# Hybrid DeltaNet and dilated-attention layer: the second half's buffers re-laid, output weight rows and the heads' K loads re-timed

## The chip, the cores and the metric

The kernel runs on one core of a Trainium2 chip. The metric is the device time in microseconds (us) of one execution; lower is better. All data are float32 in memory.

## The reference, cut to what matters

A layer on 2048 tokens of width 1024. One normalised input feeds a projection whose columns go to two mixers, a gated delta rule (4 heads of 128, chunks of 64) and a dilated sliding-window attention (8 heads of 64, three patterns); both are gated, joined, and go through one output projection into the residual stream.

```python
def hybrid_layer(x, norm_w, w_in, conv_w, a_log, dt_bias, dn_norm_w, q_norm_w, k_norm_w, rel_bias, w_out):
    h = rms_norm(x, norm_w)
    qkv_dn, z_dn, b_dn, a_dn, qkv_att, gate_att = jnp.split(h @ w_in, cuts, axis=-1)
    y_dn = deltanet_branch(qkv_dn, z_dn, b_dn, a_dn, conv_w, a_log, dt_bias, dn_norm_w)
    y_att = dilated_attention_branch(qkv_att, gate_att, q_norm_w, k_norm_w, rel_bias)
    return x + jnp.concatenate([y_dn, y_att], axis=-1) @ w_out

# attention, per pattern (window, dilation) in ((128, 1), (512, 4), (2048, 16)):
#   p = softmax(q k^T + bias) over a band of window/dilation keys, stride dilation; o = p v
# the three patterns' outputs are combined by their softmax denominators, times silu(gate)
```

## The kernel before

**Stages.** First come the normalisation, the projections and convolutions of the delta rule, and the inverses of its chunk matrices (up to about 450 us); then the delta rule, beside the attention's projections; from about 1010 us on attention itself. Every float32 product is made of three matmuls on a high and a low part (`xh`/`xl`, `wh`/`wl`, `mhh`/`mhl`): an operand is split by ScalarE (the high part, a rounding copy) and then VectorE (the low part, the difference).

**Attention in steps.** 96 steps are recorded by `step(t, gen, n)`: eight groups of 12 steps, one for each pair of heads and half of the queries, `G[0]` to `G[7]`; groups 4 to 7 (steps 48 to 95) are the second half and read all 2048 keys. A step records the scores of step t (PE `sc<-K,qz`; VectorE adds the bias and finds the minimum, `pr<-sc,bias`; ScalarE takes the exponentials `pr<-pr,ml`), the turning of the probabilities of step t-1 (PE `pt`, copied to `pT` by VectorE and ScalarE), every second step the products with the values (PE `pv<-pT,V`), and between them some matmuls of a filler. The filler is `proj_fill` (the last projections, PE `pj`) up to step 47, and `out_fill` (the output projection, PE `po<-xh,mhh` and so on) from step 48 on. `out_fill` takes its work in jobs of 24 matmuls; each starts with a `yt` tile (the delta rule's output for 128 tokens) or an `mt` tile (attention's), which PE turns and ScalarE and VectorE split into `mhh` and `mhl`.

**Loads of a group.** `load()` of a group asks for its `q1` (0.5 MB), its keys `k1` (in the trace K; 1 MB in the second half) and two `bias` tiles. It is recorded four steps before the group starts, at its second place (`at_step(b - 4, 1, ...)`). `keys(pat)` copies K into a strided tile C on GpSimd. The values come as tiles V of 256 KB, by `vload`, at fixed places of the steps.

**Output weights.** `w_out` has eight rows of blocks (128x1024, 512 KB each). Rows 0 to 3 belong to the delta rule's half: `w_out_load(k)` loads them into the two `wraw` buffers in the last projection set of `proj_fill`, rows 0 and 1 at its column block `o8 == 1`, row 2 at 4 and row 3 at 5, when a split has freed a buffer; `wo_split` splits row k at `o8 == 4 + k`. Rows 4 to 7 are asked for at the start of `out_fill`, into two `res` buffers and the two halves of the tile K1, and split while the first two jobs run.

**Buffers.** At step 48 the pools of the projections are closed and the pool `wo` opens on the same bytes; its tiles are laid out in the order in which they are first asked for: `res` (3), C1, `yt` (2), K1, then `mhh`, `mhl`, `mt`. A tile on bytes that an earlier tile had waits for the last reader of those.

**Order.** From the attention on all instructions are recorded through a small helper (line L99 in the profile) that pins each engine's instructions to the order in which the code is written. SP issues nearly all DMAs, in that order; ScalarE issues some (`qk<-qs`, `v_d<-t`). The DMAs of both take eight completion semaphores in turn, so each issue also waits for the transfer that had its semaphore eight DMAs earlier, whatever it carried.

## Time and profile before

| | |
|---|---|
| median of 3 runs | 1446.1 us (1442.88 to 1447.8) |
| the profiled execution | 1442.2 us |
| its span in the trace | 1440.4 us |
| mean granted TensorE clock | 0.987 |
| busy: PE / VectorE / ScalarE / GpSimd | 1374.0 / 897.2 / 680.1 / 427.2 us |
| moved by DMA | 205.00 MB, mean 142 GB/s |

A row of a timeline gives the start, the duration, the engine and the operation, and in brackets how long the engine was idle before it and what ended that. SPq and ACTq rows are the issuing of DMAs by those engines; how long a transfer takes to land is told by the chain of waits. PE is busy nearly all the time, so what matters are its few idle stretches and the stretches in which its granted clock is the lower of its two levels (1.2 instead of 2.4 GHz). Times of different stretches are all of one execution and add up.

### The profile page before, as it was taken

What the parts mean: (1) busy time and instruction counts of PE and PEld (TensorE: products, weight loads), DVE (VectorE), ACT (ScalarE), POOL (GpSimd) and SP (SyncE); (2) the same over time, 40 slices, a digit from 0 to 9 for tenths busy, and PEclk for the clock granted to TensorE, in tenths of its full rate; (3) what the DMA queues carried; (4) which work ended last, traced back from release to release, by engine and by line L of the source; (5) the groups of instructions that cost most, each with busy time, mean ns of one, the idle gap of its engine ahead of it and who ended that gap; (6) DMA issues with size and microseconds to landing.
All of it is one profiled execution on the core that took longest, in us unless ns stands there. A gap on an engine that the chain in (4) does not pass through costs nothing.

```text
span 1440.4 us, 28745 instructions
## 1 busy us (share of the span) xinstructions
PE 1374.0 (95%) x10234; PEld 1223.6 (85%) x10234; DVE 897.2 (62%) x2786; ACT 680.1 (47%) x1937; POOL 427.2 (30%) x499
## 2 busy tenths in 40 slices
PE   7999999999998998999999899999998999999988
PEld 7998777777877887999999889999887778888877
DVE  6526678799894365777777554544354645466455
ACT  7634436642221333444444476665555545555520
POOL 0000000000002112442432523657466274655500
PEclk9999999999999999999999999999998999999999
DMA  7653445773557556566554554464448574755764
GB/s 218 165 117 70 99 102 133 156 132 55 116 88 193 147 83 171 133 166 168 133 143 76 124 127 116 100 174 119 112 118 246 146 247 134 216 154 171 200 175 150
DMA packets 301154, 205.00 MB, mean 142 GB/s; under 512 B 149283, under 2 KB 271027, under 8 KB 300500
## 3 DMA queue, kind: packets, MB, share of 16 engines
q1 hardware_dynamic: 233924, 171.70, 48.6%
q10 hardware_dynamic: 67088, 31.47, 7.9%
q8 instruction: 81, 1.33, 0.4%
q14 instruction: 61, 0.50, 0.1%
HBM read 142.61 MB, written 60.50 MB: 141 GB/s over the span
## 4 chain that ended last, share of the span: by engine, by line
PE 61%; DVE 15%; DMA 11%; ACT 5%; issue 4%; POOL 2%; SPq 1%; ACTq 0%; DVEq 0%; POOLq 0%
PE pj L99 13%; PE po L99 8%; PE pz L99 5%; PE sc L99 5%; PE pj L206 4%; PE pj L207 4%; PE pj L208 4%; PE pv L99 3%; PE pt L99 3%; DVE cy L473 3%; DVE inv L540 2%; DMA kT<-cv 2%; PE C L714 2%; PE SU L720 2%; ACT pr L99 2%
## 5 line engine op out<-in xcount | busy, mean ns | idle before, releaser
L99 ACT ACTIVATE pr<-pr,ml 128x192 f32<-128x192 f32 (+2 forms) x384 | 156.8, 410 | 161.6 <-DVE ml L99 161.6
L99 PE MATMUL pj<-wh,xh 128*128 128x256 f32 (+1 forms) x776 | 227.7, 293 | 0.0
L99 PE MATMUL pj<-wl,xh 128*128 128x256 f32 (+1 forms) x776 | 227.6, 293 | 0.0
L99 PE MATMUL pj<-wh,xl 128*128 128x256 f32 (+1 forms) x776 | 225.8, 291 | 0.0
L208 PE MATMUL pj<-xh,wl 128*128 128x512 f32 x512 | 203.9, 398 | 3.6 <-DVE wl L192 3.6
L206 PE MATMUL pj<-xh,wh 128*128 128x512 f32 x512 | 203.9, 398 | 1.3 <-ACT cy L475 1.2
L207 PE MATMUL pj<-xl,wh 128*128 128x512 f32 x512 | 203.2, 397 | 0.0
L99 PEld LDWEIGHTS pj<-wl,xh 128*128 128x128 f32 x776 | 148.3, 191 | 0.6 <-issue 0.4
L99 PEld LDWEIGHTS pj<-wh,xl 128*128 128x128 f32 x776 | 148.3, 191 | 0.0
L99 PEld LDWEIGHTS pj<-wh,xh 128*128 128x128 f32 x776 | 148.1, 191 | 0.2
L99 DVE CUSTOM_DVE_ANT_0 pr<-sc,bias 128x192 f32<-128x192 f32 (+2 forms) x384 | 100.1, 307 | 71.0 <-PE sc L99 70.2
L208 PEld LDWEIGHTS pj<-xh,wl 128*128 128x128 f32 x512 | 96.6, 189 | 27.3 <-DVE wl L192 5.3
L206 PEld LDWEIGHTS pj<-xh,wh 128*128 128x128 f32 x512 | 96.8, 189 | 24.4 <-ACT cy L475 1.6
L473 DVE SCALAR_TENSOR_TENSOR cy<-cu,cw,cy 128x512 f32<-128x512 f32 x144 | 107.9, 752 | 15.2 <-ACT cy L471 13.6
L207 PEld LDWEIGHTS pj<-xl,wh 128*128 128x128 f32 x512 | 96.6, 189 | 21.9
L99 POOL COPY qz<-q 64x512 f32<-64x512 f32 x96 | 92.5, 964 | 57.7 <-PE sc L99 54.7
L657 POOL MEMSET at__4520<- 64x256 f32 x1 | 0.3, 304 | 354.5 <-PE pj L207 354.5
L99 DVE COPY pT<-pt 64x128 f32<-64x128 f32 (+2 forms) x220 | 69.3, 323 | 56.4 <-PE pt L99 53.1
L99 PE MATMUL po<-xh,mhh 128*128 128x512 f32 x212 | 88.8, 419 | 3.9 <-ACT mhh L99 3.9
L99 PE MATMUL pv<-pT,V 128*64 128x128 f32 (+1 forms) x1328 | 79.1, 269 | 9.8 <-DVE pT L99 4.7
L99 PE MATMUL po<-xl,mhh 128*128 128x512 f32 x212 | 88.1, 415 | 0.0
L99 PE MATMUL po<-xh,mhl 128*128 128x512 f32 x212 | 87.7, 414 | 0.3 <-DVE mhl L99 0.3
(360 smaller groups left out, 3151.8 us busy)
## 6 DMA issues: line engine op xcount, KB each, us to landing
wraw<-in_w_in SPq DMA_DIRECT2D x44, 512.0 KB, 6.9
cv<-cy ACTq DMA_DIRECT2D x48, 256.0 KB, 2.7
Fb<-F SPq DMA_DIRECT2D x64, 192.0 KB, 5.7
xr<-in_xT SPq DMA_DIRECT2D x32, 256.0 KB, 4.5
kT<-cv SPq DMA_DIRECT2D x32, 256.0 KB, 3.3
qk<-qs ACTq DMA_DIRECT2D x64, 128.0 KB, 3.3
res<-in_x SPq DMA_DIRECT2D x13, 512.0 KB, 5.2
V<-v_d SPq DMA_DIRECT2D x20, 256.0 KB, 6.2
```

The lines of the kernel that those rows point to most:

```text
L99: i = f(*args, **kw)
L206: nc.tensor.matmul(ps, wh[:, k, c * P:(c + 1) * P], xh[tb][:, kt, :], start=kt == 0, stop=False)
L207: nc.tensor.matmul(ps, wh[:, k, c * P:(c + 1) * P], xl[tb][:, kt, :], start=False, stop=False)
L208: nc.tensor.matmul(ps, wl[:, k, c * P:(c + 1) * P], xh[tb][:, kt, :], start=False, stop=kt == KT - 1)
L473: nc.vector.scalar_tensor_tensor(y, u[:, i:i + 512], cw[:, ct, i:i + 1], y, op0=ALU.mult, op1=ALU.add)
L540: nc.vector.tensor_tensor(pr_[:, :i, :i], Tt[:, :i, :i], L[:, None, :i, i].to_broadcast([P, i, i]), op=ALU.mult)
L657: nc.gpsimd.memset(at_[:CH, :, :CH], 0.0)
L714: nc.tensor.matmul(pc[:, s_], g["WQ"][:, u, s_], S0[:, s_], start=True, stop=True)
L720: nc.tensor.matmul(su[:, s_], g["Ks"][:, u, s_], VN, start=True, stop=True)
```

## The change

```diff
@@ start of the pool mid2
+    mid.tile([P, 512], F32, name="t0", bufs=2)
     rs0 = [mid.tile([P, 512], F32, name="big", bufs=3) for _ in range(2)]
     for i in range(2):
         dma(rs0[i], dap(rstd_d, i * 512, [[0, P], [1, 512]]))
@@ def wo_split(kt, raw)
         if kt < 4:
-            nc.scalar.mul(wh, raw, dnw)
-            nc.vector.scalar_tensor_tensor(wl, raw, dnw, wh.bitcast(F32), op0=ALU.mult, op1=ALU.subtract)
+            for i, r in enumerate(raw):
+                n = r.shape[1]
+                h, l = wh[:, i * n:(i + 1) * n], wl[:, i * n:(i + 1) * n]
+                nc.scalar.mul(h, r, dnw)
+                nc.vector.scalar_tensor_tensor(l, r, dnw, h.bitcast(F32), op0=ALU.mult, op1=ALU.subtract)
@@ def w_out_load(k)
-        r = wp.tile([P, 4, 260], F32, name="wraw", bufs=2).rearrange("p a b -> p (a b)")[:, :1024]
-        dma(r, w_out[k * P:(k + 1) * P, :])
-        return r
+        if k == 2:
+            rs = [mid.tile([P, 512], F32, name="big", bufs=3) for _ in range(2)]
+        else:
+            rs = [wp.tile([P, 4, 260], F32, name="wraw", bufs=2).rearrange("p a b -> p (a b)")[:, :1024]]
+        n = D // len(rs)
+        for i, r in enumerate(rs):
+            dma(r, w_out[k * P:(k + 1) * P, i * n:(i + 1) * n])
+        return rs
@@ def proj_fill()
                     if o8 == 1:
-                        rs = [w_out_load(k) for k in range(2)]
+                        rs = [w_out_load(k) for k in range(3)]
                     if o8 == 4:
                         wo_tiles(0)
                     if o8 >= 4:
                         wo_split(o8 - 4, rs[o8 - 4])
-                        if o8 < 6:
-                            rs.append(w_out_load(o8 - 2))
+                        if o8 == 4:
+                            rs.append(w_out_load(3))
@@ for i, g in enumerate(G): b = 12 * i
         if i:
-            at_step(b - 4, 1, g["load"])
+            at_step(*((b - 4, 1) if i < 4 else (b - 3, 0) if i == 4 else (b - 3, 2)), g["load"])
@@ def ring_mh()
-        return [wo.tile([P, 4, P], F32R, name="mh" + c, bufs=3) for c in "hl"]
+        t = wo.tile([P, 2, 4, P], F32R, name="mh", bufs=3)
+        return [t[:, 0], t[:, 1]]
@@ ahead of out_fill
+    wo.tile([P, 512], F32, name="mt", bufs=2)
+    C1 = wo.tile([P, S], F32, name="C1")
+    loaded = {i: half_load(Q2[i], "dn", 4) for i in range(2)}
     RAW = [wo.tile([P, D], F32, name="res", bufs=3) for _ in range(2)]
-    C1 = wo.tile([P, S + 80], F32, name="C1")[:, :S]
-    loaded = {i: half_load(Q2[i], "dn", 4) for i in range(2)}
-    K1 = wo.tile([P, S + 48], F32, name="K1")[:, :S]
+    K1 = wo.tile([P, S + 150], F32, name="K1")[:, :S]
@@ def out_fill()
-        for k in range(4):
+        def raw_load(k):
             dma(RAW[k], w_out[(4 + k) * P:(5 + k) * P, :])
+
@@ after the first job's split
+        raws = {(0, 1): (raw_load, 0), (0, 2): (raw_load, 1), (0, 12): (raw_load, 2), (0, 22): (raw_load, 3)}
+        for k, at_ in enumerate(((0, 20), (1, 8), (1, 20), (2, 8))):
+            raws[at_] = (lambda k=k: wo_split(4 + k, RAW[k]),)
@@ in the loop over a job's matmuls
-                    if nth < 2 and m in (8, 16):
-                        k = 2 * nth + m // 8 - 1
-                        wo_split(4 + k, RAW[k])
+                    if (nth, m) in raws:
+                        f, *args = raws.pop((nth, m))
+                        f(*args)
```

Five things change. (1) In the pool `mid2` the tile `t0` is laid first, so the two `rstd` loads at about 445 us go to other bytes. (2) Row 2 of `w_out` is loaded in two halves into `big` buffers, together with rows 0 and 1; row 3 is asked for at `o8 == 4`; the split of row 2 is two instructions on each engine. (3) The loads of groups 4 to 7 are recorded later: at step b-3 instead of b-4, for groups 5 to 7 at its third place. (4) The pool `wo` is laid in another order: `mt`, C1, `yt`, `res`, K1, and `mhh` and `mhl` become two halves of one tile `mh`. (5) Rows 4 to 7 are asked for and split at given matmuls of the first three jobs, the loads at matmuls 1, 2, 12 and 22 of the first job, the splits at 20 of the first, 8 and 20 of the second and 8 of the third. The order on PE and on GpSimd is the same before and after.

On SP's queue, around the end of `proj_fill` and the start of `out_fill`, before:

```order
L99 DMA wraw<-in_w_out 128x1024
L99 DMA q_12380<-qk_76 128x1024
L99 DMA K_8182<-qk_80 128x2048
L99 DMA bias<-bs_d 64x3x192 x2
L99 DMA mx_d<-gt 128x256
L99 DMA wraw<-in_w_out 128x1024
L99 DMA mx_d<-gt 128x256
L99 DMA V<-v_d 64x4x128 x2
L99 DMA mx_d<-gt 128x256
L99 DMA yt<-y_d 128x512 x2
L99 DMA V<-v_d 128x5x128
L99 DMA res<-in_w_out 128x1024 x2
```

The same place after:

```order
L99 DMA wraw<-in_w_out 128x1024
L99 DMA mx_d<-gt 128x256
L99 DMA q_12421<-qk_76 128x1024
L99 DMA K_8183<-qk_80 128x2048
L99 DMA bias<-bs_d 64x3x192 x2
L99 DMA mx_d<-gt 128x256
L99 DMA V<-v_d 64x4x128 x2
L99 DMA mx_d<-gt 128x256
L99 DMA yt<-y_d 128x512 x2
L99 DMA V<-v_d 128x5x128
L99 DMA yt<-y_d 128x512
L99 DMA ml_90<-mr 96x2x64
```

The one `wraw` load left is row 3, in row 2's old place; K stands one DMA later; the loads of rows 4 and 5 (`res<-in_w_out`) leave their place behind the first V for one three issues later, out of this piece.

On SP's queue, at the load of group 5 (q_13221 and K_12638 are its `q1` and K), before:

```order
L99 DMA V<-v_d 128x4x128
L99 DMA q_13221<-qk_77 128x1024
L99 DMA K_12638<-qk_81 128x2048
L99 DMA bias<-bs_d 64x3x192 x2
L99 DMA acc_d<-res 128x1024
L99 DMA mx_d<-gt 128x256
L99 DMA res<-in_x 128x1024
L99 DMA V<-v_d 128x4x128
L99 DMA mx_d<-gt 128x256
```

The same place after:

```order
L99 DMA V<-v_d 128x4x128
L99 DMA acc_d<-res 128x1024
L99 DMA mx_d<-gt 128x256
L99 DMA res<-in_x 128x1024
L99 DMA V<-v_d 128x4x128
L99 DMA q_13306<-qk_77 128x1024
L99 DMA K_12644<-qk_81 128x2048
L99 DMA bias<-bs_d 64x3x192 x2
L99 DMA mx_d<-gt 128x256
```

The group's four loads now stand behind the store of `acc_d`, the load of `res` and the V of the last values of group 4. Groups 6 and 7 move in the same way.

On VectorE, around the split of the last `w_out` row in the first jobs, before:

```order
L99 ISA pr,ml<-sc,bias 128x192
L99 ISA ml 128x1
L99 TENSOR_TENSOR xl_12663<-K_12638,xh_12662 128x1024
L99 COPY pT_8741<-pt 128x2x128
L99 COPY pT_8741<-pt 64x128 x2
```

The same place after:

```order
L99 ISA pr,ml<-sc,bias 128x192
L99 ISA ml 128x1
L99 COPY pT_8742<-pt 128x2x128
L99 COPY pT_8742<-pt 64x128 x2
L99 TENSOR_TENSOR xl_12665<-K_12644,xh_12664 128x1024
```

A split of a weight row that stood ahead of the copies to `pT` stands behind them; it is the split of row 7 before and of row 6 after, since each split comes about one step later.

## Rows read from the trace of the kernel before

**Rows 1.** The page, part 1: busy time, share of the span, instructions

```profile
PE 1374.0 (95%) x10234; PEld 1223.6 (85%) x10234; DVE 897.2 (62%) x2786; ACT 680.1 (47%) x1937; POOL 427.2 (30%) x499
```

**Rows 2.** Windows: stretch, its length, busy time by engine, clock, DMA share, GB/s

```profile
1080.00:1100.00 20.00, 16.97 (x154) 16.12 (x154) 8.72 (x34) 12.40 (x41) 13.02 (x16) 0.95 0.86 241
1100.00:1120.00 20.00, 17.11 (x90) 14.61 (x90) 9.40 (x37) 10.87 (x36) 13.11 (x6) 0.80 0.73 234
1160.00:1180.00 20.00, 16.70 (x125) 14.32 (x122) 5.87 (x26) 7.10 (x29) 15.65 (x17) 0.83 1.01 337
```

**Rows 3.** Timeline of PE, 1095 to 1113: start us, us, operation [idle before <-releaser]

```profile
1096.34 0.66 PE L99 MATMUL pv<-pT,V 128*64 128x128 f32 x8 [3.03 <-DVE pT L99]
...
1100.34 1.90 PE L99 MATMUL sc<-K,qz 128*128 128x192 f32 x8
...
1104.78 1.09 PE L99 MATMUL po<-cs,yt 128*128 128x128 f32 x4 [2.22 <-DMA yt<-y_d]
1106.54 0.79 PE L99 MATMUL po<-xh,mhh 128*128 128x512 f32 x1 [0.67 <-ACT mhh L99]
```

**Rows 4.** Timeline of ACT and its DMA queue, 1088 to 1108

```profile
1092.76 0.37 ACTq L99 DMA_DIRECT2D v_d<-t  x1
1093.18 1.15 ACT L99 ACTIVATE xh<-wraw,dnw 128x1024 fp32r<-128x1024 f32 x1 [3.07 <-DMA K<-qk]
...
1103.91 0.54 ACT L99 COPY pT<-pt 64x128 f32<-64x128 f32 x2
1105.91 0.58 ACT L99 CAST mhh<-po 128x512 fp32r<-128x512 f32 x1 [1.45 <-PE po L99]
```

**Rows 5.** Timeline of SP's DMA issues, 1056 to 1112

```profile
1083.21 0.42 SPq L99 DMA_DIRECT2D K<-qk  x1
...
1100.57 0.80 SPq L99 DMA_DIRECT2D yt<-y_d  x2
```

**Rows 6.** Timeline of DVE, 1086 to 1108

```profile
1094.36 1.28 DVE L99 SCALAR_TENSOR_TENSOR xl<-wraw,dnw,xh 128x1024 fp32r<-128x1024 f32 x1 [6.01 <-ACT xh L99]
```

**Rows 7.** Timeline of DVE, 1126 to 1138

```profile
1136.02 1.23 DVE L99 TENSOR_TENSOR xl<-K,xh 128x1024 fp32r<-128x1024 f32 x1 [2.10 <-ACT xh L99]
```

**Rows 8.** Timeline of PE, 1130 to 1140

```profile
1137.96 1.19 PE L99 MATMUL pv<-pT,V 128*64 128x128 f32 x16 [1.03 <-DVE pT L99]
```

**Rows 9.** Chain that ended last, 1155 to 1185: start us, us, what

```profile
1156.52 6.23 DMA Fb<-F
...
1163.33 9.41 DMA res<-in_x
```

**Rows 10.** Timeline of SP's DMA issues, 1156 to 1182

```profile
1159.97 0.38 SPq L99 DMA_DIRECT2D K<-qk  x1
...
1164.01 0.69 SPq L99 DMA_DIRECT2D V<-v_d  x1
```

**Rows 11.** Timeline of PE, 1166 to 1182

```profile
1173.61 1.13 PE L99 MATMUL pv<-pT,V 128*64 128x64 f32 x16 [3.30 <-DVE res L99]
...
1178.57 2.04 PE L99 MATMUL sc<-K,qz 128*128 128x192 f32 x8
```

**Rows 12.** Timeline of SP's DMA issues, 1222 to 1246

```profile
1226.51 0.42 SPq L99 DMA_DIRECT2D K<-qk  x1
```

**Rows 13.** Timeline of POOL, 1230 to 1246

```profile
1236.75 3.88 POOL L99 COPY C<-K 128x2048 f32<-128x2048 f32 x1 [1.01 <-DMA K<-qk]
```

**Rows 14.** Timeline of PE, 1240 to 1246

```profile
1241.67 0.69 PE L99 MATMUL pv<-pT,V 128*64 128x64 f32 x16 [1.83 <-DMA V<-v_d]
...
1244.84 1.46 PE L99 MATMUL sc<-K,qz 128*128 128x192 f32 x8
```

**Rows 15.** The page, part 6: issues, KB each, median us to landing

```profile
V<-v_d SPq DMA_DIRECT2D x20, 256.0 KB, 6.2
```

**Rows 16.** Timeline of SP's DMA issues, 440 to 452

```profile
444.30 1.76 SPq L567 DMA_DIRECT2D big<-rstd_d  x2
...
447.59 0.46 SPq L99 DMA_DIRECT2D wraw<-in_w_in  x1
```

More of the change, by code (lines that the diff above doesn't have):

```diff
@@ L1384, in split @@
                 if buf not in spare:
-                    t = wo.tile([P, S + (80 if buf == "C1" else 48)], F32R, name=buf)[:, :S]
+                    t = wo.tile([P, S + (0 if buf == "C1" else 150)], F32R, name=buf)[:, :S]
                     t = t.rearrange("p (a b k c) -> p a b k c", a=2, b=2, k=4)
```

## The prediction, made before the result

> **What bounds the kernel now.** The page's first part comes first: TensorE (PE) is busy for 1374.0 us, 95% of the span [rows 1], so every engine that is slower by itself is hidden, and time can only come out of PE's idle stretches and out of the stretches at its lower clock. The table of windows shows where those lie in the second half: of three stretches of 20 us PE was busy 16.97, 17.11 and 16.70, with a granted clock of 0.95, 0.80 and 0.83 [rows 2]. Then the timeline of PE names each idle time and what ended it, and from there the chain of waits and the timelines of ScalarE, VectorE and SP are followed back to the transfer that was late. The stretches that the change touches have five such gaps: 3.03 us ahead of the values at 1096.34, 2.22 and 0.67 at the first output job [rows 3], 1.03 at 1137.96 [rows 8], 3.30 at 1173.61 [rows 11], 1.83 at 1241.67 [rows 14]. Together 12.1 us; the clock losses come on top. After gaps of 3.03 and 3.30 the clock falls to the lower of its two levels, 1.2 GHz; a drop can also be read at 1106 behind 2.22 and 0.67, and after 1.83 at 1241.67 none can: eight score matmuls take 2.04 us behind the gap of 3.30 and 1.46 behind that of 1.83 [rows 11, 14].
>
> **Part 1, the third weight row.** The gap at 1096.34 is a chain: PE waits for `pT` on VectorE, which stands behind the low part of row 2's split (1.28 us), which had been idle for 6.01 waiting for the high part on ScalarE [rows 6]; ScalarE was idle 3.07 us until the load of K, asked for at 1083.21, had landed [rows 4, 5]. ScalarE doesn't read K. In front of the split stands its own DMA issue `v_d<-t` at 1092.76 [rows 4], and by the turn of the eight semaphores that issue had K's. So it was not the weight that came late, but an issue that stood behind 1 MB on its semaphore. In the changed kernel one more DMA shifts the turn, and the store follows a small `mx_d` store on its semaphore, long landed; and row 2 is asked for with rows 0 and 1, three column blocks sooner. ScalarE then splits right behind its `t`, about 3 us earlier, and `pT` is ready when PE comes: −3.03. The clock drop behind the gap goes with it: 0.95 over 20 us is 0.05 × 20 = 1.0 us of full-rate work lost [rows 2]: −1.0. The second half-row costs one more instruction on ScalarE and VectorE; two pieces of half the length in the place of 1.15 and 1.28 us [rows 4, 6] add some tenths there, beside PE's filler: 0. As a DMA it is issued three column blocks before its use: 0. The Trainium skill ("DMA: Bandwidth & Descriptors", section Rules for kernel authors) asks for large transfers, 1 MiB and more, and speaks against the cut in two. No row here shows that a slower transfer would be felt at that place, so by it the sum would be the same.
>
> **Part 2, the start of the output job.** `yt` is asked for at 1100.57, when the last `pj` matmul has let its bytes go, and PE waits 2.22 us for it and 0.67 for the high part [rows 3, 5]. In the new layout `yt` no longer lies on bytes that this matmul reads, so SP asks as soon as the small stores ahead of it are out. What is late next is ScalarE: its exponentials of step 48 and the copies to `pT` end at 1103.91 + 0.54 = 1104.45, and the high part `mhh` takes 0.58 behind them [rows 4], so the first product can stand at about 1105.1 instead of 1106.54: −1.5. The bounds are 0 (ScalarE is as late as `yt` was) and 2.9 (both gaps go). An idle time of some 2.7 us behind the scores stays, so I let the clock drop there stay too.
>
> **Part 3, rows 4 to 7 later.** Their splits stand behind the copies to `pT`. At 1136.02 the low part (1.23 us) stood ahead of the copy that PE waited 1.03 us for [rows 7, 8]: −1.0. Against it, a split now stands ahead of the next scores' bias instead, and may delay those by its length: two such places are new, at most 1.2 each [rows 7], so +2.5 is the bound; PE has filler matmuls there, and I take 0. The rows are used from the seventh job on; their transfers have tens of us to land: 0. Of the eight semaphores their issues wait for loads before them, which costs SP time, not PE.
>
> **Part 4, K behind V.** At group 5, `res` was asked for behind K and took 9.41 us [rows 9]; V stood behind it at 1164.01 and landed when PE started at 1173.61 [rows 10, 11], 9.5 us for 256 KB against a median of 6.2 [rows 15]. The DMA engines were full (share 1.01, 337 GB/s [rows 2]). Here the trace agrees with a statement of the Trainium skill (the same page, section Queues, rings and completion order): each engine takes descriptors in ring order, so a small load waits behind the megabyte ahead of it. With `res` and V ahead of K both land before PE wants them: −3.30. The lower clock behind the gap goes: 0.83 over 20 us is 3.4 us of lost work, of which some 0.4 fell into the gap itself: −3.0 [rows 2]. The price: K is issued at about 1163.3 instead of 1159.97 [rows 10], since `q` ahead of it still waits, on its semaphore, for the `Fb` load that landed at 1156.52 + 6.23 = 1162.75 [rows 9]. From group 6, where K was issued at 1226.51 and GpSimd waited for it until 1236.75, it takes up to 10.2 us [rows 12, 13]: here 1172.2 to 1173.5. The scores that read it stand at 1178.57 [rows 11], and 6.3 sooner once gap and clock are gone: 1172.3. So PE waits 0 to 1.2 us: +0.5.
>
> At group 6, PE waited 1.83 for the V behind K [rows 14]: −1.8. K moves from 1226.51 to about 1232, lands at about 1242, and the scores at 1244.84 come 1.8 sooner, at 1243.0: covered, by 1 us. Group 7 is built alike and has no such gap: 0.
>
> **Part 5, `t0` first.** The second `rstd` load is the second half of the issue at 444.30, so at about 445.2; its new bytes wait for a store issued shortly ahead of it, which had landed by 447.59, when another issue that waited for it went out [rows 16]. The wait is between 0 and 447.59 − 445.2 = 2.4 us; behind it on SP stand the loads for which the delta rule's start already waits, so all of it would reach PE. I take +0.5: the store went out some us earlier, and I see nothing that waited for it before.
>
> **The sum**: −3.0 − 1.0 − 1.5 − 1.0 − 3.3 − 3.0 + 0.5 − 1.8 + 0.5 = −13.6 us. Against the profiled execution (1442.2, of it 1440.4 in the span) that is 1428.6; that execution lies 3.9 below the median of the three runs, and the sum counts equally from the median: 1446.1 − 13.6 = 1432.5.
>
> **The rivals.**
> - *The clock stays up at the output job too.* Speaks for it: the remaining idle time is shorter than the 2.22 + 0.67 and the wait for `pT` before it together. The window at 1100 to 1120 loses 0.20 × 20 = 4.0 us to the clock [rows 2], about 3 of them behind 1106: 1429.5. Chance 0.2.
> - *K is late at group 5.* The Trainium skill says on the same page (Rules for kernel authors, on overlap) to issue a DMA early and wait late; the change does the opposite with the largest load. As a mechanism of this kernel: K lands 12 us after its issue, because `res` and V (0.75 MB) stand right ahead of it in the same engines; PE waits 1163.3 + 12 − 1172.3 = 3.0 us, about as long as the gap that it removed, and the clock falls as it did behind that: 6.0 − 0.5 given back. 1432.5 + 5.5 = 1438. Against it: the longest landing of K in the rows is 10.2. Chance 0.18.
> - *Hardly any change.* K is late so at group 5 and group 6 (a landing of 13 us there, 2.0 of wait and 3.0 of clock): another 5 back, 1443; or the gap at 1096 stays, since the semaphore was not its cause and the copies stand behind something else. Chance 0.12.
> - *Slower.* K lands 16 us after its issue at all three group changes. PE waits 7.0, 5 and about 4 us, each with 3 us of lower clock: 25 lost, 0.5 of it in the sum already, against 13.6 gained: 1446.1 − 13.6 + 24.5 = 1457. The point from which it decides is where the three together lose more than 14 us: waits of 2 us and a clock drop at each, a landing of about 12.7 us. For it: engines at a share of 1.01 [rows 2]. Against it: V, `res` and K together are the same bytes as before, so K should land at about the time when V did, 1173.5. Chance 0.07.
> - *The early slip is at its bound* (2.4) and the splits delay scores by 2.5: +4.4, 1437; within the range.
>
> **How the numbers follow.** The forecast 0.43, the clock 0.2, K late once 0.18, hardly any change 0.12, slower 0.07. About 0.3% (4.3 us) is what can be told from no change: faster by more than that (below 1441.8) are the first three, 0.81; within it 0.12; slower 0.07. The range from the clock's case with its bounds (1429.5, less 2.9 − 1.5 for the whole of the output job's gaps, less the 3 us by which runs differ: 1425) up to just beyond K late once with half of the early bound (1438 and 2): 1440.
>
> **What would show it.** In the profile of the changed kernel: no idle time ahead of `pv` before step 48, and `v_d<-t` issued right behind `t`; `yt` issued ahead of the last `pj`, and the first product about 4.8 us behind the first scores of step 48; the granted clock of the stretch around group 5 at 1.00; `sc<-K` of steps 60, 72 and 84 with no wait for K of over 1 us; PE's waits at the start of the delta rule no longer than before. The forecast is wrong if `sc<-K` shows a wait with K as releaser, if the first `pv` of a group still waits for V or `res`, or if a gap of the same size stands at another place in the same step.

## The result, and the profile after

The changed kernel takes 1433.5 us in the median of 7 runs (1430.11 to 1440.55), the kernel before 1446.1 (1442.88 to 1449.67): a ratio of 0.993, with a 95% interval of 0.9906 to 0.9955. A second set of runs, side by side with other kernels, gave 1429.3 against 1442.9, a ratio of 0.9907 (0.9882 to 0.9933). The ratios here and below are those on record, each with its 95% interval; they are not quotients of the medians. The forecast was 1432.5.

The windows of the changed kernel (columns as in [rows 2]; the last row is the stretch of group 6):

```profile
1080.00:1100.00 20.00, 18.41 (x170) 17.29 (x168) 11.12 (x36) 13.63 (x44) 19.31 (x18) 1.00 0.85 258
1100.00:1120.00 20.00, 17.10 (x105) 14.46 (x107) 10.73 (x43) 10.40 (x36) 9.32 (x6) 0.91 0.67 187
1160.00:1180.00 20.00, 18.66 (x158) 15.70 (x158) 9.81 (x43) 10.88 (x42) 13.65 (x13) 1.00 0.97 305
1220.00:1240.00 20.00, 20.00 (x162) 17.13 (x162) 9.07 (x42) 10.33 (x41) 12.76 (x14) 1.00 0.87 274
```

Before, the first three stretches had PE busy for 16.97, 17.11 and 16.70 us at a clock of 0.95, 0.80 and 0.83. Two of the three clock losses are gone, PE was busy 1.4 and 2.0 us longer in the first and third, and no longer in the second.

PE's waits there (timeline, columns as in [rows 3]):

```profile
1094.92 0.66 PE L99 MATMUL pv<-pT,V 128*64 128x128 f32 x8 [1.04 <-DVE pT L99]
...
1097.78 1.46 PE L99 MATMUL sc<-K,qz 128*128 128x192 f32 x8
...
1100.45 0.33 PE L99 MATMUL pt<-cs,pr 128*128 128x128 f32 x1 [0.99 <-DVE pT L99]
...
1103.67 0.80 PE L99 MATMUL po<-xh,mh 128*128 128x512 f32 x1 [2.45 <-ACT mh L99]
...
1165.72 1.15 PE L99 MATMUL pv<-pT,V 128*64 128x64 f32 x32
...
1170.42 1.54 PE L99 MATMUL sc<-K,qz 128*128 128x192 f32 x8 [1.34 <-DMA K<-qk]
```

The gap of 3.03 ahead of `pv` is one of 1.04. `yt` holds PE no longer, but there is a new gap of 0.99 ahead of a turning (1.64 in the second profile of the change), and 2.45 for the high part. At group 5 the values (1165.72) start without a wait, where 3.30 stood [rows 11], and PE now waits 1.34 for K. The gap of 1.83 at group 6 [rows 14] is gone: PE is busy 20.00 of 20 us there.

PE's instructions are the same in the same order in all kernels of this study (but for six at step 48 in one of them, named there), so the time between two of them can be compared. The table cuts the part that the change touches at seven PE instructions, named by their place; each entry is the difference of two starts in the profiled execution of a kernel. "Change again" is the changed kernel in the second set of runs, "K alone" the kernel before with part 3 alone.

| us from ... to ... | before | change | change again | K alone | forecast change | seen (first, again) |
|---|---|---|---|---|---|---|
| `pm` at 1066.46 before, to the scores of step 48 | 33.88 | 30.74 | 30.33 | 30.54 | -4.0 | -3.1, -3.5 |
| to the first output product | 6.20 | 5.89 | 6.54 | 5.35 | -1.5 | -0.3, +0.3 |
| to the product at 1148.12 before | 41.58 | 40.44 | 39.92 | 43.41 | -1.0 | -1.1, -1.7 |
| to the scores of step 60 (group 5) | 30.44 | 26.32 | 28.68 | 24.71 | -5.8 | -4.1, -1.8 |
| to the scores of step 72 (group 6) | 66.27 | 63.65 | 63.64 | 63.62 | -1.8 | -2.6, -2.6 |
| to the scores of step 84 (group 7) | 63.19 | 63.09 | 63.09 | 63.16 | 0 | -0.1, -0.1 |
| to the turning at 1364.52 before | 56.49 | 55.99 | 56.09 | 57.07 | 0 | -0.5, -0.4 |
| all of it | 298.06 | 286.12 | 288.28 | 287.85 | -14.1 | -11.9, -9.8 |

Ahead of 1066 us the profiled executions differ by up to 9 us (that instruction starts between 1063.2 and 1072.3 in the kernels below), with the same order of PE; the change's own two profiles, 1067.0 and 1064.2, lie on both sides of the kernel before, 1066.5. I take it for the spread between executions; no run shows where it comes from.

### The profile page after: what moved, and what is told of

Its sections match the earlier page's. It is cut to its first block, busy times and chain, and to the rows that moved or that the text cites. A ratio compares the mean times of both kernels' runs of the same rounds, so it can differ in the third digit from the quotient of the medians.

```text
span 1429.5 us, 28744 instructions
## 1 busy us (share of the span) xinstructions
PE 1369.7 (96%) x10234; PEld 1219.8 (85%) x10234; DVE 897.7 (63%) x2787; ACT 681.7 (48%) x1938; POOL 431.4 (30%) x499
## 4 chain that ended last, share of the span: by engine, by line
PE 65%; DVE 14%; DMA 9%; ACT 5%; issue 3%; POOL 1%; SPq 1%; ACTq 0%; DVEq 0%; POOLq 0%
PE pj L99 14%; PE po L99 9%; PE sc L99 6%; PE pz L99 5%; PE pj L206 4%; PE pv L99 4%; PE pj L207 4%; PE pj L208 4%; PE pt L99 4%; DVE cy L473 3%; DVE inv L540 2%; PE C L715 2%; PE SU L721 2%; ACT pr L99 2%; DVE inv L542 2%
## 5 line engine op out<-in xcount | busy, mean ns | idle before, releaser
L99 PE MATMUL po<-xh,mh 128*128 128x512 f32 x424 | 148.9, 414 | 6.8 <-ACT mh L99 5.8
L473 DVE SCALAR_TENSOR_TENSOR cy<-cu,cw,cy 128x512 f32<-128x512 f32 x144 | 107.9, 752 | 15.2 <-ACT cy L471 13.7
L99 POOL COPY qz<-q 64x512 f32<-64x512 f32 x96 | 96.0, 1000 | 53.0 <-PE sc L99 37.2
L99 PEld LDWEIGHTS po<-xh,mh 128*128 128x128 f32 x424 | 78.3, 189 | 20.6 <-ACT mh L99 6.5
L99 POOL TENSOR_TENSOR Fb<-Fb,op 128x256 f32<-128x256 f32 x84 | 70.0, 847 | 59.3 <-DMA Fb<-F 31.4
L99 PE MATMUL po<-xl,mh 128*128 128x512 f32 x212 | 86.8, 410 | 0.0
```

Of the source, the lines that this page charges most:

```text
L99: i = f(*args, **kw)
L473: nc.vector.scalar_tensor_tensor(y, u[:, i:i + 512], cw[:, ct, i:i + 1], y, op0=ALU.mult, op1=ALU.add)
```

## Experiments

Parts are numbered here as in the section on the change: 1 is `t0`, 2 the third weight row, 3 the loads of the groups, 4 the layout, 5 rows 4 to 7. The prediction's parts 1 to 5 are parts 2, 4, 5, 3 and 1 here.

**Part 3 alone.** The kernel before, with one line of the change:

```diff
-            at_step(b - 4, 1, g["load"])
+            at_step(*((b - 4, 1) if i < 4 else (b - 3, 0) if i == 4 else (b - 3, 2)), g["load"])
```

> The kernel before with part 3 of the change alone: the second half's groups ask for q, K and bias behind V (group 4 one place later). Theory (a small load behind the megabyte waits for it): the gap of 3.30 us at group 5 and the lower clock behind it go, the gap of 1.83 at group 6 goes, PE waits 0 to 1.5 us for K at group 5: between step 54 and step 74 the kernel gains 5 to 7 us against before. The yt gap (2.22) stays. The store v_d<-t now has q's semaphore instead of K's, so by the semaphore theory the gap of 3.03 ahead of it shrinks too, though the weight rows are loaded as before: another 1 to 4 us. In all 1435 to 1440 against 1446 for the kernel before. Rival (the gaps at groups 5 and 6 went because everything stood earlier, or through the other parts): 3.30 and 1.83 stay within 1 us, gain in all under 3 us.

Measured: 1431.97 us against 1443.06 for the kernel before, a ratio of 0.9909 (0.9881 to 0.9938). In these runs that is as much as the whole change brought in its own; side by side, further down, it is 5.7 us behind the change. The groups 5 and 6 went as expected, and better: no wait for K (`sc<-K` at 1170.84), 8.4 us gained from the product of 1148 to step 72 where 5 to 7 were expected. The wait for `yt` is still there, at 1.27. And the gap of 3.03 shrank to 0.83, though the weight rows are loaded as before. ScalarE's timeline, then PE's:

```profile
1090.52 0.37 ACTq L99 DMA_DIRECT2D v_d<-t  x1
1090.93 1.15 ACT L99 ACTIVATE xh<-wraw,dnw 128x1024 fp32r<-128x1024 f32 x1 [0.44 <-ACT t L99]
```

```profile
1094.51 0.66 PE L99 MATMUL pv<-pT,V 128*64 128x128 f32 x8 [0.83 <-DVE pT L99]
...
1101.10 0.86 PE L99 MATMUL po<-cs,yt 128*128 128x128 f32 x4 [1.27 <-DMA yt<-y_d]
1102.72 0.80 PE L99 MATMUL po<-xh,mhh 128*128 128x512 f32 x1 [0.75 <-ACT mhh L99]
...
1170.84 1.46 PE L99 MATMUL sc<-K,qz 128*128 128x192 f32 x8
```

ScalarE's store goes out at once and the split follows. In the kernel before it stood idle for 3.07 us with K as releaser [rows 4]. Group 4's K is one DMA later now, and that took its semaphore away from the store: counted in the traces, the eighth DMA ahead of the store is K in the kernel before, `q` here, and a small `mx_d` store in the changed kernel.

**The semaphore by itself.** The changed kernel, with two loads of 256 bytes behind group 4's bias, so that the store has K's semaphore again:

```diff
+            if hf and p == 0:
+                tiny = mid.tile([P, 512], F32, name="big", bufs=3)
+                for k in range(2):
+                    dma(tiny[:1, 64 * k:64 * (k + 1)], dap(rstd_d, 0, [[0, 1], [1, 64]]))
```

> The changed kernel with two loads of 256 bytes behind group 4's bias loads, into a free buffer, so that the store v_d<-t takes K's semaphore again, as in the kernel before. Row 2 of the weights is loaded as early as in the changed kernel. Theory (ScalarE stood behind its store's semaphore): ScalarE is idle for 1.5 to 3 us ahead of the split again, with K as releaser, and PE's gap ahead of the values is 2.5 to 4 us instead of 1.04: 2 to 4 us slower than the changed kernel, 1435.5 to 1437.5. Rival (row 2 came late in the kernel before): ScalarE isn't idle there, the gap stays at about 1 us, no difference beyond 0.5 us in that stretch.

Measured: 1433.59 us (0.9928, 0.9897 to 0.9959), in the median no slower than the change, against the expectation. In the stretch it is as expected: 32.74 us up to step 48 against 30.74 and 30.33. ScalarE, PE, and the window:

```profile
1089.78 0.37 ACTq L99 DMA_DIRECT2D v_d<-t  x1
1090.19 1.33 ACT L99 ACTIVATE xh<-big,dnw 128x512 fp32r<-128x512 f32 x2 [3.38 <-DMA K<-qk]
```

```profile
1093.06 0.66 PE L99 MATMUL pv<-pT,V 128*64 128x128 f32 x8 [3.04 <-DVE pT L99]
```

```profile
1080.00:1100.00 20.00, 15.32 (x140) 14.10 (x136) 9.67 (x36) 12.53 (x45) 16.89 (x16) 1.00 0.74 234
```

With the two runs before, the four combinations are complete:

| | store has K's semaphore | store has another |
|---|---|---|
| row 2 late, in `wraw` | before: ScalarE idle 3.07, PE 3.03 | K alone: 0.44, 0.83 |
| row 2 early, in `big` | this kernel: 3.38, 3.04 | change: 0.46, 1.04 |

The gap goes with the semaphore and not with the row. Having the third row early brought nothing beside that; its loads shift the turn too, as the next kernel shows. The window shows one thing more: behind this gap of 3.04 the clock in the window stayed at 1.00, where it was 0.95 behind 3.03 before [rows 2]. A gap of this length is followed by the lower clock in one execution and not in another.

**Part 3 undone.** The changed kernel with the old line for the loads.

> The changed kernel with part 3 undone: q, K and bias ahead of V again. Theory: the gap at group 5 is back at 2.5 to 4 us with a clock under 0.9 in its stretch of 20 us, that at group 6 at 1 to 2.5, the wait of 1.3 us for K is gone: 5 to 7 us slower than the changed kernel, about 1439. Rival (other parts carry it): under 2 us slower.

Measured: 1438.47 us (0.996, 0.9939 to 0.9982), where the change has 0.993 and 0.9907. PE, and the window:

```profile
1174.30 0.73 PE L99 MATMUL pv<-pT,V 128*64 128x64 f32 x16 [2.56 <-DVE res L99]
...
1240.50 0.69 PE L99 MATMUL pv<-pT,V 128*64 128x64 f32 x16 [1.32 <-DMA V<-v_d]
```

```profile
1160.00:1180.00 20.00, 17.44 (x138) 14.73 (x137) 7.71 (x37) 7.60 (x31) 15.98 (x18) 0.91 0.98 328
```

Both gaps are back, 2.56 and 1.32, with the lower clock in the stretch. From the product of 1148 to step 60 it takes 29.11 us (24.71 with part 3 alone), to step 72 then 65.09 (63.62). That is 4.2 and 1.9 us more than in the change's two profiles, where 5 to 7 were expected; its clock of 0.91 is not under 0.9. The gap ahead of step 48 does not come back (30.33 us to its scores): the store then has `q`'s semaphore, so the extra DMAs of part 2 take it away from K by themselves.

**K in two pieces.** All that the first four steps of a group read of K are its columns from 896 on:

```diff
-            dma(g["k1"], qkT_d[1][p][:, :1024 * (hf + 1)])
+            for lo, hi in ((896, 2048), (0, 896)) if hf else ((0, 1024),):
+                dma(g["k1"][:, lo:hi], qkT_d[1][p][:, lo:hi])
```

> The changed kernel with K of the second half's groups loaded as two transfers, columns 896 to 2047 first (all that the first four steps of a group read), then 0 to 895. Theory (at group 5 PE waits for K's bytes behind V's): the wait of 1.34 us ahead of the scores of step 60 goes to under 0.4, group 6 and 7 have none: 1 to 1.5 us faster between step 56 and 62. Rival (one more transfer on the same engines and semaphores costs as much, or PE waits for both pieces): the wait stays at over 1 us.

Measured: 1430.93 us (0.9926, 0.9909 to 0.9944). The wait for K is gone: 24.82 us from the product of 1148 to step 60, against 26.32 and 28.68 for the change, as good as part 3 alone. PE starts while the rest of K is still on its way: GpSimd, which copies all of K, has to wait for it until 1.38 us later. GpSimd, then PE:

```profile
1169.40 3.95 POOL L99 COPY C<-K 128x2048 f32<-128x2048 f32 x1 [1.29 <-DMA K<-qk]
```

```profile
1168.02 1.52 PE L99 MATMUL sc<-K,qz 128*128 128x192 f32 x8
```

A new wait stands behind it, at a V:

```profile
1176.38 0.69 PE L99 MATMUL pv<-pT,V 128*64 128x64 f32 x16 [0.91 <-DMA V<-v_d]
```

**K still later.**

```diff
-            at_step(*((b - 4, 1) if i < 4 else (b - 3, 0) if i == 4 else (b - 3, 2)), g["load"])
+            at_step(*((b - 4, 1) if i < 4 else (b - 3, 0) if i == 4 else (b - 2, 1)), g["load"])
```

> The changed kernel with the loads of groups 5 to 7 recorded at step b-2, second place, instead of b-3, third: one V, mt and yt more stand ahead of q and K. K is issued 4 to 6.5 us later, and took 8.6 to 10.9 us to land. Theory (K's landing is what the change pays with): PE waits 5 to 7 us for K at group 5 (1.34 in the changed kernel), 2 to 5 at group 6 and 1.5 to 4 at group 7 (0 and 0), and the lower clock follows one or more of these: 10 to 18 us slower than the changed kernel, 1443 to 1452, no better than the kernel before. Rival (with less ahead of it K lands faster, and the waits stay under 2 us each): 1434 to 1438.

Measured: 1436.75 us (0.9965, 0.9949 to 0.9982). Slower than the change, but far from what was expected. PE at group 5, and the window:

```profile
1176.43 2.37 PE L99 MATMUL sc<-K,qz 128*128 128x192 f32 x8 [2.01 <-DMA K<-qk]
```

```profile
1160.00:1180.00 20.00, 17.99 (x141) 15.11 (x140) 7.62 (x39) 9.40 (x37) 12.90 (x14) 0.92 1.02 331
```

PE waits 2.01 us at group 5, with the lower clock behind it (0.92), and not for K at groups 6 and 7. The expectation was wrong about the issue: counted from the product of 1148, K went out 17.3 us later, where the change's first profile has 15.2 and its second 17.5 with the old place in the code. SP waits here 1.4 us for a small store (`mx_d<-gt`) ahead of K, and 3.7 and 5.5 us in the change's two profiles, so most of the delay falls into time in which SP stands still in the change anyway. The scores stood 9.65 us behind the issue instead of 11.07 and 11.21. So the place in the code hardly moves K. What the profile shows as the price is 2.0 us more from step 60 to step 72 (65.68 against 63.65), where the lower clock lies; behind a wait of 2.27 in the change's second profile the clock stayed up. Of the 9.5 us between this profile and the change's first, 5.2 lie ahead of 1066 us, where the edit does not reach.

**GpSimd's copy.** The new gap of 0.99 in the changed kernel follows a slow split on VectorE; it ran beside GpSimd's copy of K. VectorE, then GpSimd, of the changed kernel:

```profile
1097.55 2.21 DVE L99 SCALAR_TENSOR_TENSOR xl<-wraw,dnw,xh 128x1024 fp32r<-128x1024 f32 x1 [2.12 <-ACT xh L99]
```

```profile
1094.76 3.91 POOL L99 COPY C<-K 128x2048 f32<-128x2048 f32 x1
```

The same split takes 1.28 with GpSimd idle (the kernel before, at 1098.96). The copy ends at 1098.67; the split ends at 1099.76, which is 1.09 later, about its own length. Two kernels move the copy:

```diff
-        at_step(b, 0, g["keys"], 1)
+        at_step(b + (i == 4), 0, g["keys"], 1)
```

> The changed kernel with GpSimd's copy C<-K of group 4 recorded one step later (step 49 instead of 48); it is needed from step 52 on. Theory (GpSimd's copy slows VectorE's split beside it, 2.21 us against 1.28 in the kernel before, where GpSimd was idle): the split of row 3 ahead of step 48 takes 1.3 us again, PE's gap of 0.99 behind it goes to under 0.3, and the first output product stands 4.7 to 5.1 us behind the first scores of step 48 instead of 5.89: about 1 us faster in that stretch, 1432.5. Rival (the split is slow for another reason, a transfer or its own operands): it takes over 2 us again, no gain.

> The changed kernel with K in two pieces, group 4's copy C<-K a step later, and the turning of the first output job recorded right behind the scores of step 48 (two pulls of the filler there instead of one, none between). Theory: the wait for K at group 5 goes (1.3 us), the gap ahead of the first product shrinks from 2.45 to under 1.5 us and stands 4.2 to 5 us behind the scores: 2 to 4 us faster than the changed kernel, about 1430.5. Rival (yt, asked for shortly ahead, now holds PE in front of its other work): the gap moves to the turning of yt, gain under 1.5 us.

The second of them also loads K in two pieces and pulls two items of the filler behind the scores of step 48 instead of one (`{48: (2, 0, 4)}`); that is the kernel with another order on PE. Measured: 1429.91 us (0.9923, 0.9908 to 0.9938) and 1429.97 us (0.9915, 0.99 to 0.9929). VectorE, GpSimd and PE of the first:

```profile
1095.57 1.29 DVE L99 SCALAR_TENSOR_TENSOR xl<-wraw,dnw,xh 128x1024 fp32r<-128x1024 f32 x1 [2.11 <-ACT xh L99]
```

```profile
1095.74 4.86 POOL L99 COPY C<-K 128x2048 f32<-128x2048 f32 x1
```

```profile
1095.81 1.46 PE L99 MATMUL sc<-K,qz 128*128 128x192 f32 x8
...
1100.77 0.79 PE L99 MATMUL po<-xh,mh 128*128 128x512 f32 x1 [2.46 <-ACT mh L99]
```

The split took 1.29, the gap of 0.99 is gone, and the first product stands 4.96 us behind the scores, as expected. But the copy was not clear of the split: GpSimd doesn't wait for the steps here, it only does two `qz<-q` copies more ahead of K's. The copy started 0.17 us behind the split, and took 4.86 instead of 3.91. In the second kernel it started 0.46 us ahead:

```profile
1095.06 4.51 DVE L99 SCALAR_TENSOR_TENSOR xl<-wraw,dnw,xh 128x1024 fp32r<-128x1024 f32 x1 [2.11 <-ACT xh L99]
```

```profile
1094.60 3.89 POOL L99 COPY C<-K 128x2048 f32<-128x2048 f32 x1
```

```profile
1100.27 0.33 PE L99 MATMUL pt<-cs,pr 128*128 128x128 f32 x1 [2.86 <-DVE pT L99]
1102.90 0.80 PE L99 MATMUL po<-xh,mh 128*128 128x512 f32 x1 [2.31 <-ACT mh L99]
```

There the split took 4.51 and PE waited 2.86: the first product came 7.61 us behind the scores, worse than before the change, and the gap ahead of it is 2.31 where under 1.5 was expected. Whichever starts first holds the other off until about its end: 1094.60 + 3.89 = 1098.49 is the copy's end, and 1095.06 + 4.51 − 1.28 = 1098.29 is where the split can have begun. It is so in all fourteen profiles, from 1075 to 1160 us: eleven splits of a whole row start behind such a copy, and ten of them end 1.08 to 1.09 us after it (one 2.07); seven start first and take 1.23 to 1.29 us, and the copy takes 4.5 to 4.9 instead of 3.7 to 4.0. The Trainium skill ("SBUF — State Buffer", section SBUF: two separate sides) states this: VectorE and GpSimd share one pair of ports, an exclusive lock that the one that starts first holds for its whole instruction, where the VectorE instruction has two inputs in SBUF, as the split has, and GpSimd reads SBUF. The trace agrees, in both directions.

**Both, with the copy two steps later** (step 50).

> The changed kernel with K in two pieces (columns 896 to 2047 first) and group 4's copy C<-K recorded two steps later (step 50), clear of the split of row 3 on VectorE. Theory (VectorE's split waits until a GpSimd copy that started first has ended): the split takes 1.3 us whoever is early, the gap of 0.99 ahead of step 48's last turning goes, the first output product stands 4.7 to 5.1 us behind the scores, and the wait of 1.34 for K at group 5 is gone: 2 to 3 us faster than the changed kernel beside it. Rival: the copy meets another split and the time comes back there: within 1 us.

Measured: 1432.60 us (0.9926, 0.9906 to 0.9947); the change beside it 1429.28 (0.9907, 0.9882 to 0.9933). VectorE, then GpSimd:

```profile
1097.87 1.28 DVE L99 SCALAR_TENSOR_TENSOR xl<-wraw,dnw,xh 128x1024 fp32r<-128x1024 f32 x1 [2.11 <-ACT xh L99]
```

```profile
1098.05 4.86 POOL L99 COPY C<-K 128x2048 f32<-128x2048 f32 x1
```

The times in the stretch are as expected: 4.97 us from the scores to the first product, 24.81 from the product of 1148 to step 60, no wait for K. But the copy is not clear of the split. It stands at the same place among GpSimd's instructions as one step later, and again it started just behind the split, by 0.18 us, so whether the split is safe when the copy is early was not tested. All of the table's part takes 285.82 us, 0.3 and 2.5 less than in the change's two profiles. The median is 3.3 us above the change's and the intervals overlap: no gain can be told.

**The new layout of the second half's buffers alone.** The kernel before with part 4.

> The kernel before with the new layout of the second half's buffers alone (mt, C1, yt, res, K1, one mh tile). Theory: yt is asked for 5 us or more sooner, PE's wait of 2.22 for it goes, and the first output product stands 4.5 to 5.5 us behind the first scores of step 48 instead of 6.2, held by ScalarE: 1 to 2 us faster than before up to step 50, the rest as before: about 1444.5. Rival: the wait for the high part takes all of it, 0.

Measured: 1446.52 us against 1443.06, 1.0005 (0.9981 to 1.003). The median shows no gain; the profile is of the longest of the ten runs (1453.0 us). The first product stands 4.50 us behind the scores, as expected. Then more than that is lost again, 45.26 us to the product of 1148 instead of 41.58. VectorE and PE:

```profile
1115.48 4.48 DVE L99 TENSOR_TENSOR xl<-res,xh 128x1024 fp32r<-128x1024 f32 x1 [1.73 <-ACT xh L99]
...
1125.33 2.78 DVE L99 TENSOR_TENSOR xl<-res,xh 128x1024 fp32r<-128x1024 f32 x1 [2.11 <-ACT xh L99]
```

```profile
1128.83 1.19 PE L99 MATMUL pv<-pT,V 128*64 128x128 f32 x16 [2.42 <-DVE pT L99]
...
1139.64 1.57 PE L99 MATMUL sc<-C,qz 128*128 128x192 f32 x8 [2.24 <-DVE ml L99]
```

Now it is the splits of rows 4 and 5 that GpSimd's copies hold off, 4.48 and 2.78 us for work of 1.23, ahead of the copies that PE waits for. What starts sooner meets another collision here.

**Part 5 undone.** The changed kernel, with rows 4 to 7 asked for ahead of the first job and split ahead of the copies, as before.

> The changed kernel with part 5 undone: rows 4 to 7 asked for before the first output job, their splits at products 8 and 16 of the first two jobs, ahead of the copies to pT, as in the kernel before. Theory: PE waits for pT behind a split again at one place or two, 1.0 us each, and where GpSimd's copy C<-K has started first the split holds everything behind it for up to 4 us: 1 to 4 us slower than the changed kernel, the loss between steps 48 and 54. Rival (PE's filler hides it): within 0.5 us in that stretch.

Measured: 1432.35 us (0.993, 0.9907 to 0.9952). The change beside it has 1429.28, 3.1 us less, with overlapping intervals. From the first product to that of 1148 this kernel takes 41.50 us instead of 40.44 and 39.92, and the gap of 1.03 [rows 8] is back, as expected:

```profile
1135.19 1.19 PE L99 MATMUL pv<-pT,V 128*64 128x128 f32 x16 [1.03 <-DVE pT L99]
```

But the gap is not what makes the difference. The stretch itself as one window (columns as in [rows 2]), in the kernel before, the change, and this kernel:

```profile
1106.54:1148.12 41.58, 39.29 (x256) 33.56 (x257) 26.70 (x96) 23.64 (x79) 14.40 (x12) 0.94 0.58 160
1103.67:1144.11 40.44, 38.43 (x257) 32.73 (x257) 24.98 (x88) 23.19 (x77) 14.21 (x11) 0.96 0.59 169
1103.87:1145.37 41.50, 39.24 (x256) 33.51 (x257) 26.68 (x96) 23.63 (x79) 13.83 (x11) 0.94 0.47 125
```

PE is idle 2.29, 2.01 and 2.26 us in it; the rest of the difference is the clock, 0.94, 0.96 and 0.94. Where part 5 takes the gap of 1.03 away, PE waits for VectorE at the end of the stretch, which it doesn't do without part 5:

```profile
1144.11 0.50 PE L99 MATMUL po<-xh,mh 128*128 128x512 f32 x1 [0.61 <-DVE mh L99]
```

And the four kernels with part 5 whose window at 1100 to 1120 shows a clock of 0.83, as it does here, take 40.9 to 41.6 us for the stretch. So part 5 saves at most 0.5 us of idle time, and what goes beyond that is the clock. From the product of 1148 to step 60 this kernel takes 24.70 us, without a wait for K, against 26.32 and 28.68: what the change gains ahead of that product is waited away at group 5.

**The change and part 3 alone, side by side.**

> The changed kernel itself, beside the others of this call. Theory: 1430 to 1436, with PE's waits as before it: 1.0 ahead of the values before step 48, 2.4 ahead of the first product, 1.0 to 1.6 for K at group 5.

> The kernel before with part 3 alone, again, beside the whole change in one call. Theory (K behind V, and the semaphore turn that moves with it, carry the gain; the other parts give and take within 2 us): the same time as the whole change within 2 us. Rival: the other parts bring 3 us or more, and this one is that much slower.

Measured: 1429.28 us (0.9907) and 1434.97 (0.9943, 0.9922 to 0.9964). PE in this profile of the change, which waited for K longer than the first, and longer than the 1.0 to 1.6 us expected:

```profile
1154.56 1.19 PE L99 MATMUL pv<-pT,V 128*64 128x128 f32 x16 [1.14 <-DVE pT L99]
...
1169.66 1.54 PE L99 MATMUL sc<-K,qz 128*128 128x192 f32 x8 [2.27 <-DMA K<-qk]
```

And in part 3 alone, VectorE and GpSimd at a split of row 4:

```profile
1108.26 4.61 DVE L99 TENSOR_TENSOR xl<-res,xh 128x1024 fp32r<-128x1024 f32 x1 [1.95 <-ACT xh L99]
```

```profile
1108.06 3.72 POOL L99 COPY C<-K 128x2048 f32<-128x2048 f32 x1
```

Here the change is 5.7 us ahead, more than the 2 us of the expectation: by the medians its rival holds, that the other parts bring 3 us or more. But the intervals overlap, and the table's part is equal in the two profiles, 288.28 and 288.21. In the first runs, which were not side by side, part 3 alone had the lower ratio, 0.9909 against 0.993. So what the other parts bring together is between nothing and 5 us in the medians, 0 to 2 in the stretch, and stays open at that.

The two profiles of part 3 alone have nearly the same gaps at the output job (1.27 and 0.75, then 1.40 and 0.86 us), but not the same clock behind them. The window at 1100 to 1120 in the first and in the second:

```profile
1100.00:1120.00 20.00, 18.14 (x104) 15.27 (x106) 9.50 (x32) 11.20 (x37) 13.26 (x7) 0.83 0.77 244
1100.00:1120.00 20.00, 16.28 (x106) 12.94 (x106) 12.86 (x34) 11.01 (x37) 13.21 (x8) 1.00 0.74 244
```

## Why the prediction was right, point by point

- *The third row and the gap ahead of step 48* (−3.0 and −1.0 of clock): seen −3.1 to −3.5. The cause was read rightly, the store on K's semaphore; the four combinations show it. But the prediction gave it to the third weight row alone, and the later loads bring it as well, since they move K by one DMA. "`pT` is ready when PE comes" was wrong: 0.6 to 1.0 us stay. Part of that is the split, which took 1.70 and 1.76 us beside GpSimd's `qz<-q` copies instead of 1.28; the rest is not explained.
- *The start of the output job* (−1.5): this term was mis-sized, −0.3 and +0.3. Its step, that the exponentials and copies end at 1104.45 and `mhh` follows, took ScalarE's times of before as fixed. ScalarE waits for VectorE, and VectorE's split waits for GpSimd's copy: 2.21 and 2.87 us in the change's two profiles instead of 1.28. Where the split starts first the step holds: 4.96 and 4.97 us against the forecast 4.8.
- *Rows 4 to 7 behind the copies* (−1.0): seen −1.1 and −1.7, and the undoing brought +1.1 to +1.6. The size fits by luck. The gap of 1.03 went, but PE's idle time in the stretch fell by only 0.3 and 0.5 us, because VectorE is late elsewhere: the wait ahead of the scores of step 54 went from 1.25 to 1.39 us, and 0.61 and 0.40 us are waited for `mh` at the end. These delays were set at 0. The other 0.9 and 1.2 us are the clock, which this term did not count. The second profile has one more new wait behind the stretch, 1.14 for `pT`, shown above.
- *K behind V at group 5* (−5.8): the gap and the lower clock behind it went, but K costs more than the 0.5 that was taken: 1.34 and 2.27 us. The landing was forecast at 8.9 to 10.2 us; it took 10.94:

```profile
1159.35 10.94 DMA K<-qk
```

  K was issued at 1159.35, behind `res`, V and `q`, in a stretch with the DMA engines at 0.97. That is 15.2 us behind the product of 1148, as forecast (1163.3 − 1148.1), and 17.5 in the second profile. Part 3 alone, where PE needs 3 us longer to that product (in its first profile a wait of 2.27 ahead of the scores of step 54, and a clock of 0.90), has no wait for K. K's issue hardly follows PE: it stands 60.8 to 63.9 us behind the scores of step 48 in all kernels with part 3, whether PE reaches the product of 1148 after 44.9 us or after 49.1. So what is saved ahead of K's issue is in part lost again in front of K. Ahead of it SP waits 3.7 and 5.5 us for a store `mx_d<-gt` in the change's two profiles, 1.3 in the kernel before; why that store lands late is not shown. The rival of a late K at one place was half right: the place and the releaser, but 1.3 to 2.3 us, with the clock still at 1.00.
- *Group 6* (−1.8) and *group 7* (0): −2.6 and −0.1. The 0.8 more at group 6 is for the most part the end of the slow stretch behind group 5: the eight score matmuls of step 60 took 2.04 us before and 1.54 now.
- *The early wait* (+0.5): the issue of the two `rstd` loads took 2.94 us instead of 1.76 [rows 16], so the wait is there. But it does not reach PE, where the prediction had all of it arrive: in all ten profiles with `t0` first the issue took 2.9 to 3.3 us, in the four without 1.4 to 1.8, and PE's gap behind it was 3.4 to 4.7 in the ten and 3.7 to 4.7 in the four. So no cost can be told apart. The changed kernel's row:

```profile
447.18 2.94 SPq L568 DMA_DIRECT2D big<-rstd_d  x2
```

- *The sum*: −14.1 was forecast for the table's part, −11.9 and −9.8 were seen there; the medians moved by 12.6 and 13.6. So the total fits the forecast better than its terms do. The output job was forecast too large by 1.2 to 1.8 us and group 5 by 1.7 to 4.0, clock included; the clock behind the output job, group 6 and the last stretch gave back some of it unforeseen. That the median came within 1 us of 1432.5 is in part luck: one kernel's runs alone spread over 9 to 10 us.
- *The rivals*: the clock staying up at the output job came true in part: 0.91 in both profiles of the change instead of 0.80 [rows 2]. But it is no sure effect of the change: behind the same gap of 2.45 us ahead of the first product the window shows 0.91 in five profiles and 0.83 in four. Slower (K late by 16 us) was out of reach: the longest chain from K's issue to its landing was 11.08 us and the largest wait for K 2.27.

## What to carry to other kernels

A wait's releaser can be a transfer that the waiting engine doesn't read: look at which earlier DMA holds its semaphore, and count the DMAs between the two. Ahead of a large load put the small ones that are needed sooner, and then expect the large one to be the next wait: gains upstream of its use count in full only if its issue comes sooner too. When a stretch gets shorter by the length of a gap that was removed, read its idle time and its clock apart before the gap is given the credit. An edit that brings a VectorE split forward must be checked against what GpSimd does at that moment.

## What the runs showed of the hardware

- A VectorE instruction that reads two tiles of SBUF (a split of 1.23 to 1.28 us) took up to 4.61 beside a GpSimd copy of 3.7 to 3.9 us that had started first, 0.2 us ahead (1108.06 and 1108.26); started first itself, by 0.17 us, it took 1.29 and the copy 4.86. A few tenths of a microsecond decide over 3 us.
- Behind gaps of 3.03 and 3.04 ahead of the same instruction the granted clock of the window was 0.95 in one kernel and 1.00 in the other. In the same kernel, part 3 alone, nearly the same gaps were followed by 0.83 in one execution and by 1.00 in another. A clock loss that was read behind one gap is no fixed price of its length.
- At group 5, where PE waited for it, K (1 MB) was read 9.4 to 11.2 us behind its issue, with the DMA engines at a share of 0.91 to 1.02 in the window.
